# Rotary embedding on a quarter of each head: a partition that holds two runs of 8 rows instead of one of 16, with tables of 8 rows

## The chip, the cores and the metric

One core of a Trainium2 chip runs the kernel. The metric is the device time of one execution in microseconds (us); less is better. Work is spread over the engines of the core (here VectorE, called DVE in the profile, does all the arithmetic; SyncE, called SP, and GpSimd, called POOL, issue transfers) and over 16 DMA engines that move data between the device's main memory (HBM) and the 128 partitions of on-chip memory.

## What is computed

The input `x` has shape 16 x 512 x 16 x 64 (batch, sequence, heads, dim) in float32, 33.6 MB. The first 32 of the 64 values of each head are rotated, the last 32 are passed through. `cos` and `sin` have 512 x 32 values, of which the first 16 columns are used.

```python
def reference(x, cos, sin):
    batch, seq, heads, dim = x.shape
    half_dim = dim // 2
    x1, x2 = (x[..., :half_dim].copy(), x[..., half_dim:].copy())
    cos = cos[None, :, None, :].copy()
    sin = sin[None, :, None, :].copy()
    rotated_first = x1[..., :half_dim // 2] * cos[..., :half_dim // 2] - x1[..., half_dim // 2:] * sin[..., :half_dim // 2]
    rotated_second = x1[..., :half_dim // 2] * sin[..., :half_dim // 2] + x1[..., half_dim // 2:] * cos[..., :half_dim // 2]
    return np.concatenate([rotated_first, rotated_second, x2], axis=-1).astype(np.float32)
```

## The kernel before

A row is one position of one sequence: 16 heads x 64 values, 4 KB. There are 16 x 512 = 8192 rows. The kernel cuts them into T = 4 tiles of 2048 rows (8.4 MB each); in a tile, each of the 128 partitions holds K = 16 consecutive rows, 64 KB that are contiguous in HBM (`xf` and `of`, lines 36 and 37). A ring of three tile slots (`ring`, line 45) holds the tiles in on-chip memory. A tile is loaded whole, its first halves of the heads are rotated in place, and the slot is stored whole: so all of `x`, the part that passes through too, goes in and out once. Tile 3 takes the slot of tile 0 after the store of tile 0.

All loads are issued from SP's queue, and the stores of tiles 0, 1 and 3 too; the store of tile 2 is issued from POOL's. Each queue keeps its program's order. On SP this order is: load 0, load 1, the upper half (rows 8 to 15 of each partition) of load 2; then store 0, the lower half of load 2, load 3, store 1, store 3. Store 1 is held back by a dependency written by hand (lines 118 to 123) until the rotation named `near`, rows 0 to 4 of tile 2, is done. An issue on SP that has to wait holds back those behind it.

The tables: 512 positions are 32 groups of 16 rows, so partition p needs the cos and sin of group p mod 32. Two transfers from POOL's queue put the 32 groups of cos and sin on every fourth partition of `stage` (lines 62 to 64, after a memset of the columns that are read). VectorE then builds `table` on all 128 partitions: one shuffle within blocks of 32 partitions (line 73), four copies that gather the 32 groups on partitions 0 to 31 (`packed`, line 80), and four copies that write them to the four blocks of 32 partitions, each value block doubled (line 83). `C` and `Sn` are views of `table`.

`rotate(t, lo, hi)` (line 90) treats rows lo to hi of every partition of tile t with four VectorE instructions: x1 times sin into a temporary `b_t` (line 96), x1 times cos in place (97), a subtraction on the first 16 values (98) and an addition on the next 16 (101). It is called twice per tile with 8 rows, three times for tile 2 (8, 5 and 3 rows). A rotation waits for the load of its rows as a whole.

Of the kernel before, what the change touches and what calls it, by code (L numbers as in the profile page):

```python
# [1 line left out]

# [4 lines left out]


@with_exitstack
def kernel(  # L10
    ctx: ExitStack,
    tc: tile.TileContext,
    x: bass.AP,
    cos: bass.AP,
    sin: bass.AP,
    out: bass.AP,
):
    nc = tc.nc
    fp32 = mybir.dt.float32
    P = 128  # L20
    B, S, H, D = x.shape
    Q = D // 4
    HF = D // 2

    K = 16
    T = B * S // (P * K)
    PB = S // K
    REP = P // PB  # L30
    R = H * D
    NS = 3
    KC = K // 2
    KM = 5

    xf = x.rearrange("b s h d -> (b s h d)").rearrange("(t p f) -> t p f", t=T, p=P)
    of = out.rearrange("b s h d -> (b s h d)").rearrange("(t p f) -> t p f", t=T, p=P)
    cosf = cos.rearrange("(p k) j -> p (k j)", k=K)
    sinf = sin.rearrange("(p k) j -> p (k j)", k=K)

    const_pool = ctx.enter_context(tc.tile_pool(name="const", bufs=1))
    b_pool = ctx.enter_context(tc.tile_pool(name="bp", bufs=1, space=bass.MemoryType.PSUM))


    ring = const_pool.tile([P, NS, K, H, D], fp32)
    stage = const_pool.tile([P, 2, K, HF], fp32)
    spun = const_pool.tile([P, 2 * K, Q], fp32)
    packed = const_pool.tile([PB, 2 * K, Q], fp32)
    table = const_pool.tile([P, 2, K, 2, Q], fp32)

    def rows(t, lo, hi):
        return ring[:, t % NS, lo:hi].rearrange("p k h d -> p (k h d)")

    def load(t, lo=0, hi=K):
        return nc.sync.dma_start(out=rows(t, lo, hi), in_=xf[t, :, lo * R : hi * R])

    def store(t, lo=0, hi=K, queue=nc.sync):
        return queue.dma_start(out=of[t, :, lo * R : hi * R], in_=rows(t, lo, hi))  # L58


    nc.vector.memset(stage[:, :, :, 0:Q], 0.0)  # L61
    spread = stage.rearrange("(j b) t k i -> j b t (k i)", b=REP)
    nc.gpsimd.dma_start(out=spread[:, 0, 0], in_=cosf)  # L63
    nc.gpsimd.dma_start(out=spread[:, 0, 1], in_=sinf)  # L64
    load(0)
    load(1)
    load(2, KC, K)

    PQ = PB // REP
    nc.vector.stream_shuffle(  # L73
        out=spun[:],
        in_=stage.rearrange("p t k j -> p (t k) j")[:, :, 0:Q],
        mask=[j % PQ * REP for j in range(PB)],
    )
    for q in reversed(range(REP)):
        n = PQ * (q + 1)
        nc.vector.tensor_copy(out=packed[0:n], in_=spun[q * PB : q * PB + n])  # L80

    for r in range(REP):
        nc.vector.tensor_copy(  # L83
            out=table[r * PB : (r + 1) * PB].rearrange("p t k c j -> p (t k) c j"),
            in_=packed.unsqueeze(2).to_broadcast((PB, 2 * K, 2, Q)),
        )
    C = table[:, 0].rearrange("p k c j -> p k (c j)")
    Sn = table[:, 1].rearrange("p k c j -> p k (c j)")

    def rotate(t, lo, hi):  # L90
        x1 = ring[:, t % NS, lo:hi, :, 0:HF]
        c = C[:, lo:hi].unsqueeze(2).to_broadcast((P, hi - lo, H, HF))
        s = Sn[:, lo:hi].unsqueeze(2).to_broadcast((P, hi - lo, H, HF))
        b_full = b_pool.tile([P, KC, H, HF], fp32, name="b_t")
        b_t = b_full[:, 0 : hi - lo]
        nc.vector.tensor_mul(out=b_t, in0=x1, in1=s)  # L96
        nc.vector.tensor_mul(out=x1, in0=x1, in1=c)  # L97
        nc.vector.tensor_sub(  # L98
            out=x1[:, :, :, 0:Q], in0=x1[:, :, :, 0:Q], in1=b_t[:, :, :, Q:HF]
        )  # L100
        return nc.vector.tensor_add(  # L101
            out=x1[:, :, :, Q:HF], in0=x1[:, :, :, Q:HF], in1=b_t[:, :, :, 0:Q]
        )

    rotate(0, 0, KC)
    rotate(0, KC, K)
    store(0)
    load(2, 0, KC)
    load(3)
    rotate(1, 0, KC)  # L110
    rotate(1, KC, K)
    behind_loads = store(1)
    rotate(2, KC, K)
    near = rotate(2, 0, KM)
    rotate(2, KM, KC)
    store(2, queue=nc.gpsimd)

    tc.add_manual_dep(
        behind_loads.ins,
        near.ins.name,  # L120
        mybir.DependencyInfo(mybir.DependencyClass.Sync, mybir.DependencyReason.DATA),
        reason="the store follows the loads at the DMA engines",
    )
    rotate(3, 0, KC)
    rotate(3, KC, K)
    store(3)


# [1 line left out]
_INS = ['x', 'cos', 'sin']  # L130
_OUTS = [((16, 512, 16, 64), 'float32')]


# [23 lines left out]
```

## Time and profile before

| | |
|---|---|
| median of 3 runs | 161.76 us (161.6 to 161.9) |
| span of the profiled execution | 159.5 us |
| VectorE busy | 112.9 us, 47 instructions |
| GpSimd busy | 1.9 us |
| data moved | 67.24 MB, mean 422 GB/s |
| rotation of 8 rows on VectorE | 4.43 + 4.42 + 2.29 + 2.28 us |
| first rotation starts, last one ends | 23.03 us, 131.2 us |

The span is the time from the first to the last instruction of one profiled execution. The times of the runs are taken without the profiler and hold some 2 us more. In the profile a line such as `49.92 0.35 SPq L58 DMA_DIRECT2D out_dram<-ring  x1` gives the start, the length, the queue, the line of the kernel, the operation and what goes where; the length of such an issue is that of the instruction, not of the transfer. The view of the DMA queues gives, for each queue (q1 is SP's, q0 is POOL's), the number of packets, the MB and the time that its packets took as a share of 16 engines over the stretch asked for; a packet is counted in the stretch in which it starts, so a short stretch can show over 100%. Each transfer also ends with one 4-byte packet per DMA engine that reports its end: the 176 packets under 512 B are those of 11 transfers.

### The profile page before, as it was taken

Reading aid. Unit: us, or ns where it says so; the run is one execution under the profiler, and the core shown is the slowest. Engines: PE = TensorE matmul, PEld = TensorE weight load, DVE = VectorE, ACT = ScalarE, POOL = GpSimd, SP = SyncE. Lnnn points to the kernel's source line nnn. Section 1 sums busy time; section 2 is a strip of 40 time slices with the busy share of each in tenths; the row PEclk is TensorE's granted clock in tenths of the full one; section 3 lists DMA queues with packets and bytes.
Section 4 is the critical chain, followed back from the end, with each engine's and each line's share of the span. In section 5 each row is a group of like instructions: output and inputs, shape, how many; then the busy total and the mean of one; then the engine's idle time right before and its main releaser. Section 6 shows DMA issues by size and latency. Waiting matters only on the chain.

```text
span 159.5 us, 115 instructions
## 1 busy us (share of the span) xinstructions
DVE 112.9 (71%) x47; POOL 1.9 (1%) x7
## 2 busy tenths in 40 slices
DVE  1000959999999999999999999999999990000000
POOL 3000000000000000000000000010000000000000
DMA  7969979799699699699996996996996997999966
GB/s 263 542 263 542 444 345 526 345 444 526 271 493 551 279 510 526 263 394 411 510 526 263 526 526 263 526 526 263 526 526 263 526 460 329 526 394 394 526 263 263
DMA packets 1360, 67.24 MB, mean 422 GB/s; under 512 B 176, under 2 KB 176, under 8 KB 208
## 3 DMA queue, kind: packets, MB, share of 16 engines
q1 hardware_dynamic: 1152, 58.72, 85.7%
q0 software_dynamic: 208, 8.52, 12.4%
HBM read 33.69 MB, written 33.55 MB: 422 GB/s over the span
## 4 chain that ended last, share of the span: by engine, by line
DVE 61%; DMA 14%; issue 5%; DVEq 1%
DVE b_t L96 22%; DVE ring L97 22%; DMA ring<-in_x_dram 14%; DVE ring L101 10%; DVE ring L98 7%; DVEq L152 1%; DVEq L96 0%
## 5 line engine op out<-in xcount | busy, mean ns | idle before, releaser
L96 DVE TENSOR_TENSOR b_t<-ring,table 128x4096 f32<-128x4096 f32 (+2 forms) x9 | 35.6, 3959 | 2.1 <-DMA ring<-in_x_dram 1.8
L97 DVE TENSOR_TENSOR ring<-ring,table 128x4096 f32<-128x4096 f32 (+2 forms) x9 | 35.5, 3950 | 0.3
L98 DVE TENSOR_TENSOR ring<-ring,b_t 128x2048 f32<-128x2048 f32 (+2 forms) x9 | 18.4, 2049 | 0.3
L101 DVE TENSOR_TENSOR ring<-ring,b_t 128x2048 f32<-128x2048 f32 (+2 forms) x9 | 18.4, 2043 | 0.0
L73 DVE LOAD_MASK_SELECT spun<-stage x1 | 0.0, 14 | 14.4 <-DMA stage<-in_sin_dram 14.4
L83 DVE COPY table<-packed 32x1024 f32<-32x1024 f32 x4 | 2.7, 684 | 0.1
L58 POOL DMA_DIRECT2D out_dram<-ring x1 | 0.6, 562 | 101.7 <-DVE ring L101 101.7
L80 DVE COPY packed<-spun 32x512 f32<-32x512 f32 (+3 forms) x4 | 1.7, 416 | 0.1
L61 DVE MEMSET stage<- 128x512 f32 x1 | 0.5, 485 | 0.9 <-PEq L141 0.9
L73 DVE STREAM_SHUFFLE spun<-stage 128x512 f32<-128x512 f32 x1 | 0.7, 721 | 0.0
L63 POOL DMA_DIRECT2D stage<-in_cos_dram x1 | 0.6, 644 | 1.3 <-DVE stage L61 1.3
L64 POOL DMA_DIRECT2D stage<-in_sin_dram x1 | 0.5, 535 | 0.0
L141 POOL MEMSET const-bfloat16-1.0<- 128x1 bf16 x1 | 0.1, 102 | 0.0
L141 POOL MEMSET const-float32-0.0<- 128x1 f32 x1 | 0.1, 99 | 0.2 <-issue 0.2
L141 POOL MEMSET const-float32-1.0<- 128x1 f32 x1 | 0.1, 99 | 0.0
L141 POOL MEMSET const-uint8-127<- 128x1 uint8 x1 | 0.1, 99 | 0.0
## 6 DMA issues: line engine op xcount, KB each, us to landing
ring<-in_x_dram SPq DMA_DIRECT2D x2, 4096.0 KB, 40.7
stage<-in_cos_dram POOLq DMA_DIRECT2D x1, 64.0 KB, 9.0
stage<-in_sin_dram POOLq DMA_DIRECT2D x1, 64.0 KB, 13.3
ring<-in_x_dram SPq DMA_DIRECT2D x3, 29.0
out_dram<-ring SPq DMA_DIRECT2D x3, 27.4
out_dram<-ring POOLq DMA_DIRECT2D x1, 39.5
```

Source lines behind the costliest of these rows:

```text
L58: return queue.dma_start(out=of[t, :, lo * R : hi * R], in_=rows(t, lo, hi))
L61: nc.vector.memset(stage[:, :, :, 0:Q], 0.0)
L63: nc.gpsimd.dma_start(out=spread[:, 0, 0], in_=cosf)
L64: nc.gpsimd.dma_start(out=spread[:, 0, 1], in_=sinf)
L73: nc.vector.stream_shuffle(out=spun[:], in_=stage.rearrange("p t k j -> p (t k) j")[:, :, 0:Q], mask=[j % PQ * REP for j in range(PB)],)
L80: nc.vector.tensor_copy(out=packed[0:n], in_=spun[q * PB : q * PB + n])
L83: nc.vector.tensor_copy(out=table[r * PB : (r + 1) * PB].rearrange("p t k c j -> p (t k) c j"), in_=packed.unsqueeze(2).to_broadcast((PB, ...
L96: nc.vector.tensor_mul(out=b_t, in0=x1, in1=s)
L97: nc.vector.tensor_mul(out=x1, in0=x1, in1=c)
L98: nc.vector.tensor_sub(out=x1[:, :, :, 0:Q], in0=x1[:, :, :, 0:Q], in1=b_t[:, :, :, Q:HF])
L101: return nc.vector.tensor_add(out=x1[:, :, :, Q:HF], in0=x1[:, :, :, Q:HF], in1=b_t[:, :, :, 0:Q])
L152: with _tile.TileContext(nc) as tc:
```

## The change

A partition now holds, of each tile, two runs of K = 8 rows: a tile is still 2048 rows, but it is cut into two halves of 1024 rows (4 MB), and partition p holds rows 8p to 8p+7 of each half. In HBM the two runs of a partition lie 4 MB apart, and adjacent partitions 32 KB apart instead of 64 KB. In on-chip memory the layout of a slot is as large as before (`[P, NS, NI, K, H, D]` with NI = 2).

Since 8 x 64 = 512, partition p now needs the table of group p mod 64, and both runs of a partition need the same one. The tables have 8 rows on 64 partitions: the transfers put 64 groups of 1 KB on every second partition of `stage`; memset and shuffle work on half the elements; `packed` and its four copies are gone. Five copies build `table`: for each of the two blocks of 32 groups, one of 32 and one of 16 partitions straight from the shuffled tile, and at last one from partitions 0 to 63 to 64 to 127.

The whole-tile loads and stores carry both runs of each partition in one transfer (128 x 2 x 8192 values); the two half loads of tile 2 now carry one run each. The rotations have the same sizes and the same order, and so do the issues on both queues.

```diff
-    K = 16
-    T = B * S // (P * K)
+    K = 8
+    NI = 2
+    T = B * S // (P * K * NI)
     PB = S // K
-    REP = P // PB
+    G = 32
...
-    xf = x.rearrange("b s h d -> (b s h d)").rearrange("(t p f) -> t p f", t=T, p=P)
-    of = out.rearrange("b s h d -> (b s h d)").rearrange("(t p f) -> t p f", t=T, p=P)
+    xf = x.rearrange("b s h d -> (b s h d)").rearrange("(t i p f) -> t p i f", t=T, i=NI, p=P)
+    of = out.rearrange("b s h d -> (b s h d)").rearrange("(t i p f) -> t p i f", t=T, i=NI, p=P)
...
-    ring = const_pool.tile([P, NS, K, H, D], fp32)
+    ring = const_pool.tile([P, NS, NI, K, H, D], fp32)
...
-    packed = const_pool.tile([PB, 2 * K, Q], fp32)
...
-    def rows(t, lo, hi):
-        return ring[:, t % NS, lo:hi].rearrange("p k h d -> p (k h d)")
+    def runs(t, lo, hi):
+        return ring[:, t % NS, lo:hi].rearrange("p i k h d -> p i (k h d)")
 
-    def load(t, lo=0, hi=K):
-        return nc.sync.dma_start(out=rows(t, lo, hi), in_=xf[t, :, lo * R : hi * R])
+    def load(t, lo=0, hi=NI):
+        return nc.sync.dma_start(out=runs(t, lo, hi), in_=xf[t, :, lo:hi])
 
-    def store(t, lo=0, hi=K, queue=nc.sync):
-        return queue.dma_start(out=of[t, :, lo * R : hi * R], in_=rows(t, lo, hi))
+    def store(t, lo=0, hi=NI, queue=nc.sync):
+        return queue.dma_start(out=of[t, :, lo:hi], in_=runs(t, lo, hi))
...
-    spread = stage.rearrange("(j b) t k i -> j b t (k i)", b=REP)
+    spread = stage.rearrange("(m b) t k i -> m b t (k i)", b=2)
     nc.gpsimd.dma_start(out=spread[:, 0, 0], in_=cosf)
     nc.gpsimd.dma_start(out=spread[:, 0, 1], in_=sinf)
     load(0)
     load(1)
-    load(2, KC, K)
+    load(2, 1, 2)
...
-        mask=[j % PQ * REP for j in range(PB)],
+        mask=[j % (G // 2) * 2 for j in range(G)],
     )
-    for q in reversed(range(REP)):
-        n = PQ * (q + 1)
-        nc.vector.tensor_copy(out=packed[0:n], in_=spun[q * PB : q * PB + n])
-
-    for r in range(REP):
-        nc.vector.tensor_copy(
-            out=table[r * PB : (r + 1) * PB].rearrange("p t k c j -> p (t k) c j"),
-            in_=packed.unsqueeze(2).to_broadcast((PB, 2 * K, 2, Q)),
-        )
+    flat = table.rearrange("p t k c j -> p (t k) c j")
+    for g in range(PB // G):
+        for q, n in ((2 * g + 1, G), (2 * g, G // 2)):
+            nc.vector.tensor_copy(
+                out=flat[g * G : g * G + n],
+                in_=spun[q * G : q * G + n].unsqueeze(2).to_broadcast((n, 2 * K, 2, Q)),
+            )
+    nc.vector.tensor_copy(out=flat[PB:P], in_=flat[0:PB])
...
-    def rotate(t, lo, hi):
-        x1 = ring[:, t % NS, lo:hi, :, 0:HF]
+    def rotate(t, i, lo=0, hi=K):
+        x1 = ring[:, t % NS, i, lo:hi, :, 0:HF]
...
-    load(2, 0, KC)
+    load(2, 0, 1)
     load(3)
-    rotate(1, 0, KC)
-    rotate(1, KC, K)
+    rotate(1, 0)
+    rotate(1, 1)
     behind_loads = store(1)
-    rotate(2, KC, K)
-    near = rotate(2, 0, KM)
-    rotate(2, KM, KC)
+    rotate(2, 1)
+    near = rotate(2, 0, 0, KM)
+    rotate(2, 0, KM, K)
     store(2, queue=nc.gpsimd)
...
```

More of the change, by code (lines that the diff above doesn't have):

```diff
@@ L23 @@
     HF = D // 2
-    K = 16
-    T = B * S // (P * K)
+    K = 8
+    NI = 2
+    T = B * S // (P * K * NI)
     PB = S // K
-    REP = P // PB
+    G = 32
     R = H * D
     NS = 3
-    KC = K // 2
     KM = 5
-    xf = x.rearrange("b s h d -> (b s h d)").rearrange("(t p f) -> t p f", t=T, p=P)
-    of = out.rearrange("b s h d -> (b s h d)").rearrange("(t p f) -> t p f", t=T, p=P)
+    xf = x.rearrange("b s h d -> (b s h d)").rearrange("(t i p f) -> t p i f", t=T, i=NI, p=P)
+    of = out.rearrange("b s h d -> (b s h d)").rearrange("(t i p f) -> t p i f", t=T, i=NI, p=P)
     cosf = cos.rearrange("(p k) j -> p (k j)", k=K)
@@ L66 @@
     load(1)
-    load(2, KC, K)
-    PQ = PB // REP
+    load(2, 1, 2)
     nc.vector.stream_shuffle(
@@ L75 @@
         in_=stage.rearrange("p t k j -> p (t k) j")[:, :, 0:Q],
-        mask=[j % PQ * REP for j in range(PB)],
+        mask=[j % (G // 2) * 2 for j in range(G)],
     )
-    for q in reversed(range(REP)):
-        n = PQ * (q + 1)
-        nc.vector.tensor_copy(out=packed[0:n], in_=spun[q * PB : q * PB + n])
-    for r in range(REP):
-        nc.vector.tensor_copy(
-            out=table[r * PB : (r + 1) * PB].rearrange("p t k c j -> p (t k) c j"),
-            in_=packed.unsqueeze(2).to_broadcast((PB, 2 * K, 2, Q)),
-        )
+    flat = table.rearrange("p t k c j -> p (t k) c j")
[6 more added lines that the diff above has]
+    nc.vector.tensor_copy(out=flat[PB:P], in_=flat[0:PB])
     C = table[:, 0].rearrange("p k c j -> p k (c j)")
     Sn = table[:, 1].rearrange("p k c j -> p k (c j)")
-    def rotate(t, lo, hi):
-        x1 = ring[:, t % NS, lo:hi, :, 0:HF]
+    def rotate(t, i, lo=0, hi=K):
+        x1 = ring[:, t % NS, i, lo:hi, :, 0:HF]
         c = C[:, lo:hi].unsqueeze(2).to_broadcast((P, hi - lo, H, HF))
         s = Sn[:, lo:hi].unsqueeze(2).to_broadcast((P, hi - lo, H, HF))
-        b_full = b_pool.tile([P, KC, H, HF], fp32, name="b_t")
+        b_full = b_pool.tile([P, K, H, HF], fp32, name="b_t")
         b_t = b_full[:, 0 : hi - lo]
@@ L103, in rotate @@
         )
-    rotate(0, 0, KC)
-    rotate(0, KC, K)
+    rotate(0, 0)
+    rotate(0, 1)
     store(0)
-    load(2, 0, KC)
+    load(2, 0, 1)
     load(3)
-    rotate(1, 0, KC)
-    rotate(1, KC, K)
+    rotate(1, 0)
+    rotate(1, 1)
     behind_loads = store(1)
-    rotate(2, KC, K)
-    near = rotate(2, 0, KM)
-    rotate(2, KM, KC)
+    rotate(2, 1)
+    near = rotate(2, 0, 0, KM)
+    rotate(2, 0, KM, K)
     store(2, queue=nc.gpsimd)
@@ L123 @@
     )
-    rotate(3, 0, KC)
-    rotate(3, KC, K)
+    rotate(3, 0)
+    rotate(3, 1)
     store(3)
```

## The prediction

> **What bounds the kernel now.** I read the page first: the engine table, the 40 slices and the DMA queues.
>
> ```profile
> span 159.5 us, 115 instructions
> DVE 112.9 (71%) x47; POOL 1.9 (1%) x7
> DMA packets 1360, 67.24 MB, mean 422 GB/s; under 512 B 176, under 2 KB 176, under 8 KB 208
> q1 hardware_dynamic: 1152, 58.72, 85.7%
> q0 software_dynamic: 208, 8.52, 12.4%
> ```
>
> The two queues hold the 16 DMA engines for 85.7 + 12.4 = 98.1% of the span, 156.5 of 159.5 us. The 3.0 us left over lie at the two ends: no packet starts before 1.75 us, and after the last packets (started at 155.5 to 156.0, 2.4 us long) come the last landing and the closing barrier. VectorE is busy for 71% only. So this kernel is one unbroken DMA stream, although the chain of waits puts 61% of the span on VectorE: that chain ends at the last VectorE instruction (131 us) and does not follow the queue of stores behind it. What happens on VectorE counts only where it makes a DMA issue too late to keep the stream unbroken. So I looked next at the timeline, for the start and the issues:
>
> ```profile
> 0.74 1.33 SPq L55 DMA_DIRECT2D ring<-in_x_dram  x3
> 15.83 0.01 DVE L73 LOAD_MASK_SELECT spun<-stage  x1 [14.43 <-DMA stage<-in_sin_dram]
> ...
> 18.41 2.78 DVE L83 COPY table<-packed 32x1024 f32<-32x1024 f32 x4
> 23.03 4.43 DVE L96 TENSOR_TENSOR b_t<-ring,table 128x4096 f32<-128x4096 f32 x1 [1.85 <-DMA ring<-in_x_dram]
> ...
> 49.92 0.35 SPq L58 DMA_DIRECT2D out_dram<-ring  x1
> ...
> 98.90 32.68 SPq L58 DMA_DIRECT2D out_dram<-ring  x2
> ```
>
> The tables are complete at 21.2 us, and VectorE then idles 1.85 us until load(0) has landed: the first rotation starts on the load, not on the tables. Store(0) is issued at 49.92 us, store(1) at 98.90, store(3) at 131.24.
>
> Last I asked for the packets of single stretches, because the changed kernel makes its transfers of other pieces. The trace already holds both sizes: a whole tile goes as 128 packets of 64 KB (one per partition), and each half of tile 2 as 128 packets of 32 KB. The first two rows below are stretches with whole tiles only (24 to 41 us and 82 to 97 us), the third one with the first half of tile 2 only (43 to 50 us); columns are packets, MB, share of 16 engines.
>
> ```profile
> q1 hardware_dynamic: 112, 7.34, 99.6%
> ...
> q1 hardware_dynamic: 96, 6.29, 96.7%
> ...
> q1 hardware_dynamic: 87, 2.85, 94.2%
> ```
>
> Packets are counted where they start. A 64 KB packet takes 0.996 x 17 x 16 / 112 = 2.4188 us, and 0.967 x 15 x 16 / 96 = 2.4175 us; I take 2.418. A 32 KB packet takes 0.942 x 7 x 16 / 87 = 1.2127 us. Two of them take 2.4254, that is 7 ns more than one of 64 KB (5 to 10 ns with the rounding of the shares). That is the only price of the smaller piece that this trace shows.
>
> **The change part by part.**
>
> *Tables (off the path).* Removed on VectorE: four copies of about 0.416 us into packed (1.66) and four of 0.684 into table (2.74). The memset and the shuffle work on half the elements (0.485 and 0.721 us before). Added: five copies of 512 elements, each between half of 0.684 (0.34) and the 0.418 of the 32x512 copy, 1.7 to 2.1 us in all. Some 2.3 to 2.7 us of copies go, and up to 0.6 us of shuffle and memset. All of that falls in the wait for load(0), so it is worth nothing: VectorE idles longer. Even if the sin table landed no earlier than now (15.83), the tables would be ready by 15.83 + 0.72 + 2.1 = 18.7, 4.3 us ahead of the load. The table transfers become 64 rows of 1 KB instead of 32 rows of 2 KB, the same 128 KB; their whole share today is 32 packets of 4 KB, about 0.3 us per engine, and I see no reason for a change above 0.1. They probably land earlier, as they take turns with 32 KB packets instead of 64 KB ones. That too is hidden.
>
> *Rotations.* Same forms, same order, same count: 0.
>
> *Loads and stores of whole tiles.* Seven issues (loads 0, 1, 3; stores 0 to 3) x 128 partitions / 16 = 56 packets of 64 KB per engine become 112 of 32 KB. The two halves of tile 2 keep one run per partition. Cost: 56 x 7.2 ns = 0.40 us, straight on the end, since the stream has no gap that could take it. Bounds: 0, if two runs of a partition travel as one packet; 0.28 to 0.56 by the rounding; 0.82 by the other half of tile 2, whose reads follow the stores (71.5 to 79 us: 96 packets, 97.3%, 1.2163 us each, so 56 x 14.6 ns). No row shows a 32 KB store, but a 64 KB store is priced like a load (140 to 157 us: 112 packets, 99.7%, 2.421 us), so I give both the same. I take 0.40, since most of the packets follow packets of their own direction.
>
> *The 4 MB between two runs.* No row shows such a step. The nearest ones are tiles whose partitions lie 64 KB apart, on which 16 engines read and write at 2.418 us per packet without a slow one, so the memory side has room: 0. From far above, each jump could cost what the first packets of the run cost (below, 0.75 us): 56 x 0.75 = 42 us. I take 0, because adjacent partitions are already separate requests at 64 KB steps, and pay nothing.
> The Trainium skill speaks against the change here: "DMA: Bandwidth & Descriptors", section "Latency and other measured facts", reports copies whose partitions lie a large power of two apart, with 207 GB/s at 512 KB and 103 at 4 MB. Taken at its word, the 135 us of whole-tile packets would double, an estimate of some 297 us from that page. But its distance is that between partitions, which here shrinks from 64 to 32 KB; no run here shows a 4 MB one.
>
> *Issues.* The order on SP and on POOL stays: loads 0, 1, half of 2; store 0; other half; load 3; stores 1 and 3 on SP; tables and store 2 on POOL. Each whole-tile issue now describes 256 runs, not 128. SP's five load issues take 0.33 to 0.43 us now. Whether that grows is not shown; between 0 and a doubling, +0.35 us. What matters is when the stream needs the next issue:
> - Start: issue at 0.74, first packets at 1.75 to 2.6. Any growth counts in full.
> - Store(0): issue at 49.92; the last half-tile packets end, and its own start, at 50.9 to 51.7. The lead is about 1.0 us, as at the start, so there is hardly any slack today. Load end moves by 16 x 7 ns = 0.11 later, VectorE (through load(0)'s landing) by 8 x 7 = 0.06: slack grows 0.05.
> - Store(1): issue at 98.90 behind the rotation marked near; its packets start at 99.8 to 100.3, where the loads end. Load end moves 32 x 7 = 0.23, VectorE 0.06: slack grows 0.17.
> - Load(3) (71.72) is covered by the half of tile 2 that runs until 80.5; store(2) on POOL (issue 0.56 us) by store(1), alone good for 19 us; store(3) (131.24) by store(2)'s packets, up to about 143. No cost there, and nothing else waits behind them.
> I take 0, because POOL's issues do not go by the runs they describe: 0.54 to 0.64 us for a table of 32, 0.56 for a store of 128.
>
> **Sum**: the profiled 159.5 + 0.40 = 159.9 us. The median of the runs is 161.76, 2.26 above that span; the same offset gives 162.16, rounded 162.2.
>
> **The rivals.**
> - *Nothing changes* (the two runs travel together, or the 7 ns hide): 161.8. For it: 7 ns is near the rounding of the view. Against: the half-tile stretches show each run of 32 KB as a packet of its own.
> - *Later issues*: describing two runs per partition takes SP 0.35 us longer, and the stream breaks at the start (0.35), at store(0) (0.35 - 0.05) and at store(1) (0.35 - 0.17). For it: both leads are only about 1 us. Against: POOL's rows. 162.16 + 0.83 = 163.0.
> - *Memory side*: 4 MB steps slow some packets. At the price of the read-after-write row, 162.6; further up the sum has no row but the 42 us, 204.
> - *Faster, through the start.* The first 16 packets take 372.5% x 0.85 us = 3.17 us each instead of 2.42, 0.75 us of excess on every engine. If that belongs to the length of the first request and vanishes with shorter ones, 161.76 + 0.40 - 0.75 = 161.4. It shows as faster only if nearly all of it goes. Against: this looks like the delay to the first data, which any length pays.
>
> **How the numbers follow.** My forecast (0.40, give or take 0.2: 161.95 to 162.4) gets 0.57, nothing 0.14, later issues 0.15, the memory side 0.06, faster 0.08. 0.2% is 0.32 us, about what a measurement of this kernel tells from no change: slower begins at 162.08, faster below 161.44. The lower edge of the forecast falls within; so faster 0.08, same 0.22, slower 0.70. The range goes from 161.6 (nothing, less the 0.16 by which runs lie under the median) to 163.1 (later issues, with 0.1 of scatter); it leaves out most of the faster case and the upper part of the memory one.
>
> **What would show it.** Right: q1 has 1152 + 6 x 128 = 1920 packets, q0 208 + 128 = 336; whole-tile stretches give 1.213 us per packet; the shares sum to about 98% of a span near 159.9; the first rotation still starts near 23.1 behind load(0), with over 4 us of idle in front. Wrong: packets of 64 KB still (nothing); windows around 1.75, 51 or 100 us in which less than 16 engines are at work (later issues); packets clearly above 1.22 us in mid-stream (memory side); first packets under 1.5 us (faster). An issue on SP well over 0.43 us would make the second rival likely.

## The result, and the profile after

The changed kernel takes 163.49 us (median of 4 runs, 163.02 to 164.04), the kernel before 161.68 us (161.54 to 161.9, 4 runs): a ratio of 1.0117, 95% interval 1.0095 to 1.014. It is slower, as forecast, but by 1.8 us and not by 0.4, and outside the range that was given (161.6 to 163.1). A second set of 6 runs gave 163.83 us (163.19 to 164.51) and 1.0137 (1.0117 to 1.0158). The runs of the changed kernel also scatter over 1.5 us, those of the kernel before over some 0.6.

The page of the changed kernel, with the engine table and the DMA queues:

```profile
span 160.9 us, 112 instructions
DVE 110.1 (68%) x44; POOL 2.1 (1%) x7
DMA packets 2256, 67.24 MB, mean 418 GB/s; under 512 B 176, under 2 KB 176, under 8 KB 208
q1 hardware_dynamic: 1920, 58.72, 85.5%
q0 software_dynamic: 336, 8.52, 12.3%
```

The reader sees the packet counts that were forecast (1920 and 336: each whole-tile packet has become two), and the same kind of kernel: 97.8% of 160.9 us on the DMA queues, 157.3 us instead of 156.5. The span is 1.42 us longer, so 0.8 us of it is packet time and some 0.6 us is not.

The timeline of the changed kernel, at its start and at the issues on SP:

```profile
10.99 0.01 DVE L69 LOAD_MASK_SELECT spun<-stage  x1 [9.86 <-DMA stage<-in_sin_dram]
...
13.29 0.42 DVE L81 COPY table<-table 64x512 f32<-64x512 f32 x1
23.09 4.43 DVE L91 TENSOR_TENSOR b_t<-ring,table 128x4096 f32<-128x4096 f32 x1 [9.39 <-DMA ring<-in_x_dram]
...
49.98 0.39 SPq L57 DMA_DIRECT2D out_dram<-ring  x1
...
98.97 32.72 SPq L57 DMA_DIRECT2D out_dram<-ring  x2
```

The tables are complete at 13.7 us instead of 21.2 and the first rotation starts at 23.09 instead of 23.03: all that the shorter table work gained is waiting for load 0 (9.39 us of idle in front of the rotation instead of 1.85). The issues are 0.06 to 0.07 us later. None of this is a loss of more than that.

Where packets do nothing but follow each other, they cost what the half tile had shown. The queue view of the changed kernel from 110 to 128 us, where stores 1 and 2 take turns (packets, MB, share of 16 engines):

```profile
q0 software_dynamic: 127, 4.16, 53.5%
q1 hardware_dynamic: 113, 3.70, 47.6%
```

1.011 x 18 x 16 / 240 = 1.213 us for 32 KB. Over the run, 112 packets of 1.213 instead of 56 of 2.418 make 0.45 us.

The rest stands at one place, the turn from store 0 to the half load of tile 2 that is queued behind it. First the kernel before, the last packet of store 0 on each of the 16 engines (67.5 to 69 us); then the changed kernel, the same packets (69.3 to 70.5 us) and, next, the first packets of the half load (71 to 72.6 us, with 16 end-of-transfer packets of 7 to 9 ns among the 32):

```profile
q1 hardware_dynamic: 16, 1.05, 184.3%
```

```profile
q1 hardware_dynamic: 16, 0.52, 141.4%
...
q1 hardware_dynamic: 32, 0.52, 97.3%
```

In the kernel before, a last packet takes 1.843 x 1.5 = 2.76 us, 0.35 above 2.418. In the changed one it takes 1.414 x 1.2 = 1.70 us, 0.48 above 1.213, and the first reads take 0.973 x 1.6 = 1.56 us, 0.34 above. I summed, from the packet records, all time above the standing price (2.418 and 1.213 us) in packets that start between 60 and 77 us: 0.41 us per engine in the kernel before (0.43 in a second trace), 0.86 in the changed one (1.11 in a second). This sum is called "the turn" below. In no other stretch does the excess come to more than 0.05 us per engine, but for the first packets of the run (0.75 before, 0.66 after).

The last term is at the end. The stretches of the kernel before and of the changed one in which the last packets start (us, length, busy VectorE, busy GpSimd, clock, DMA share, GB/s):

```profile
155.50:156.50 1.00, 0.00 (x0) 0.00 (x0) 1.00 2.42 1049
156.50:157.50 1.00, 0.00 (x0) 0.00 (x0) 1.00 0.00 0
```

```profile
156.00:157.00 1.00, 0.00 (x0) 0.00 (x0) 1.00 1.06 459
157.00:158.00 1.00, 0.00 (x0) 0.00 (x0) 1.00 1.14 492
158.00:159.00 1.00, 0.00 (x0) 0.00 (x0) 1.00 0.31 131
```

Before, all 16 last packets start in one stretch (1049 GB/s for 1 us are 16 x 64 KB). After, 4 engines (131 GB/s are 4 packets of 32 KB) start theirs after 158 us, the other twelve before. By the end-of-transfer packets, the last engine ends 0.62 us after the mean of the 16, before 0.14. The trace lines up as: packets +0.45, turn +0.45, uneven end +0.48, first packet 0.06 later; in all 1.44 of 1.42 us. What is left out nearly cancels. The engines also stand still at the turn, 0.23 us per engine between 71 and 72.5 us (in the kernel before under 0.01). Against that, each packet starts 3 to 4 ns before the one ahead of it has ended, which happens 56 times more often (some -0.2), and the first packets of the run are 0.09 us cheaper.

The second trace of the changed kernel (span 162.3 us) shows the uneven end more plainly:

```profile
157.00:158.00 1.00, 0.00 (x0) 0.00 (x0) 1.00 1.06 459
158.00:159.00 1.00, 0.00 (x0) 0.00 (x0) 1.00 0.38 164
159.00:160.00 1.00, 0.00 (x0) 0.00 (x0) 1.00 0.08 33
```

One packet of 32 KB is 33 GB/s for 1 us: one engine alone is still at work, 1.89 us after the mean. Its own packets can be followed back one by one: at the turn its last store packet takes 2.29 us, it stands still for 0.41 us, and its first read takes 2.27 us: 2.5 us lost within 5 us. It never makes them up: behind 81 us all 16 engines have about 64 packets of 32 KB left, the late one as many as the others. When the others change to store 1 at 100 us it loses another 0.6 us on its last two reads. Of the 2.83 us by which this trace is longer than that of the kernel before, the uneven end makes 1.74, the slow packets at the turn 0.70 and the smaller pieces 0.45 (the rest -0.06): in this slower run the late engine is the main term.

### The profile page after: what moved, and what is told of

The parts are those of the page before. It is cut to its first block, busy times and chain, and to the rows that moved or that the text cites. A ratio compares the mean times of both kernels' runs of the same rounds, so it can differ in the third digit from the quotient of the medians.

```text
span 160.9 us, 112 instructions
## 1 busy us (share of the span) xinstructions
DVE 110.1 (68%) x44; POOL 2.1 (1%) x7
## 3 DMA queue, kind: packets, MB, share of 16 engines
q1 hardware_dynamic: 1920, 58.72, 85.5%
## 4 chain that ended last, share of the span: by engine, by line
DVE 61%; DMA 14%; issue 5%; DVEq 1%
DVE b_t L91 22%; DVE ring L92 22%; DMA ring<-in_x_dram 14%; DVE ring L96 10%; DVE ring L93 7%; DVEq L147 1%; DVEq L91 0%
## 5 line engine op out<-in xcount | busy, mean ns | idle before, releaser
L77 DVE COPY table<-spun 32x512 f32<-32x512 f32 (+1 forms) x4 | 1.7, 417 | 0.1
```

What stands on the lines that cost most here:

```text
L77: nc.vector.tensor_copy(out=flat[g * G : g * G + n], in_=spun[q * G : q * G + n].unsqueeze(2).to_broadcast((n, 2 * K, 2, Q)),)
```

## Experiments

Each run is compared with the kernel before on the same chip (161.56 to 161.70 us there). "Last engine" is its end after the mean of the 16 in the trace of that run. In the diffs, names are those of the kernel before unless the changed kernel is meant, and only the lines that matter are shown ("..." between them). In e9, e13, e14, e15 and e17 tile 0 is rotated in the order upper half, lower half.

**The changed kernel again, and three versions of where its runs lie.**

> The changed kernel once more, for the scatter and a second trace. In its first trace the extra time stands in three terms: 32 KB packets at 1.213 us instead of 64 KB ones at 2.418 (0.45 us), slow packets at the turn from store 0 to the reads of tile 2 at 69 to 73 us (a mean of 0.85 us per DMA engine instead of 0.41), and an uneven end (last engine 0.61 us after the mean instead of 0.14). If the slow turn belongs to the kernel, this trace shows it again: 0.7 to 1.8 us per engine of excess there, and times of 162.8 to 164.2 us. If it was chance in one execution, the excess falls to about 0.4 and the time to about 162.3.

Measured (e1): 163.83 us, turn 1.11, last engine 1.89 us. The slow turn belongs to the kernel. How uneven it leaves the engines differs from run to run (last engine 0.62 us late at 163.09 us, 1.89 at 164.51), which fits the scatter.

```diff
+    PAD = 16
-    ring = const_pool.tile([P, NS, K, H, D], fp32)
+    ring = const_pool.tile([P, NS, 2, KC * R + PAD], fp32)
```

> The kernel before with 16 unused values between the two halves of a slot, so that each partition's 64 KB travel as two 32 KB pieces that are adjacent in HBM; rows, tables and order as before. Theory A (the size of the piece does it all): 32 KB packets at 1.213 us, a slow turn of 0.7 to 1.2 us per engine, 163.0 to 164.0 us, like the changed kernel. Theory B (the 4 MB between the runs makes the turn slow, the size only its 0.45 us): turn at about 0.4 us, 162.1 to 162.3 us.

Measured (e2): 163.98 us (1.0155, 1.0135 to 1.0174), turn 1.01, last engine 1.68. Some 0.4 us of the time is something else: an issue for slots with a gap takes 0.60 to 0.66 us on SP, and the first packet comes at 2.21 us instead of 1.75 (in e10 and e14 too, at 2.17 and 2.18).

```diff
-        return nc.sync.dma_start(out=runs(t, lo, hi), in_=xf[t, :, lo:hi])
+        for i in range(lo, hi):
+            nc.sync.dma_start(out=runs(t, i, i + 1), in_=xf[t, :, i : i + 1])
...
-    rotate(0, 0)
     rotate(0, 1)
+    rotate(0, 0)
```

> The changed kernel with every whole-tile transfer cut into two of 4 MB, one for each run, so that no transfer alternates between places 4 MB apart; packets stay at 32 KB and partitions 32 KB apart. Tile 0 is rotated in the order second run, first run, so that VectorE starts after the whole of load 0 as before. Theory A (size of the piece): turn still 0.7 to 1.2 us per engine, 163.0 to 164.0 us. Theory B (the alternation over 4 MB): turn back at about 0.4 us, 162.2 to 162.5 us (0.45 for the packets, at most 0.1 for the added end-of-transfer packets).

Measured (e3): 164.35 us (1.017, 1.0157 to 1.0183), turn 1.02, last engine 1.02. It also lost 0.8 us at 92 to 94 us, which I had not planned: the first half of store 2 went out from POOL at 90.74 us, while load 3 was still running.

```diff
-    load(2, 1, 2)
+    load(2, 0, 1)
...
-    load(2, 0, 1)
+    load(2, 1, 2)
```

> The changed kernel with the two half loads of tile 2 exchanged: the first run is loaded at the start, the second one behind store 0. Only the addresses at the turn change, by 4 MB. Theory A and theory B both expect no difference (162.8 to 164.2 us, turn 0.7 to 1.8 us). A third theory C, that particular addresses of the read and the written tile collide at the turn, expects another turn: 0.4 us or less, or clearly over 1.8, and a time at least 0.4 us away from the changed kernel's.

Measured (e4): 163.27 us (163.09 to 164.78), turn 1.02, last engine 1.62.

What follows: the 4 MB between the runs is without effect. With adjacent runs (e2) the loss is as large, and without alternation (e3) too. Moving the addresses at the turn by 4 MB (e4) leaves the turn at 1.02; the median of e4 is 0.56 us below that of e1, less than the runs of either scatter. Theory B and theory C fall; the cause is in cutting the transfers into smaller pieces.

**Which pieces: store 0, the reads behind it, or the other tiles.** In e6 the slots of tiles 1 and 2 have the gap of e2, the slot of tiles 0 and 3 has none; e10 is the reverse.

```diff
-    store(0)
+    store(0, 0, KC)
+    store(0, KC, K)
```

> The kernel before with store 0 alone cut into two transfers of 32 KB pieces; all else in 64 KB as before. Theory A1 (the pieces of the store that comes right ahead of the turn make it slow): turn of 0.7 to 1.2 us per DMA engine, a last engine 0.4 to 2 us behind the mean, 162.2 to 163.9 us. Theory A2 (small pieces everywhere are needed, for instance because they leave the engines in another state long before the turn): turn at 0.4 us, 161.5 to 161.9 us.

Measured (e5): 162.77 us (1.0071, 1.0058 to 1.0084), but the turn from store 0 to the reads is 0.00; the loss lies at the other end of store 0. The view of SP's issues in this run, and the queue view for 50 to 51 us, the last packets of the loads ahead of store 0:

```profile
36.55 13.79 SPq L58 DMA_DIRECT2D out_dram<-ring  x2
```

```profile
q1 hardware_dynamic: 16, 0.52, 204.5%
```

The first half of store 0 is issued as soon as half of tile 0 is rotated, 14 us before the loads ahead of it are through. Their last packets take 2.05 us each instead of 1.213, on all engines alike. The kernel before issues store 0 at 49.92 us, 1.0 us before its first packet, and its loads end at full speed. This run mixed two things and settles neither theory. It shows one thing more: the reads behind store 0 are issued as early as in the kernel before (50.39 us, before 50.31), and the turn to them costs nothing.

```diff
+    whole = const_pool.tile([P, 2, KC * R], fp32)
+    split = const_pool.tile([P, NS - 1, 2, KC * R + PAD], fp32)
```

> The kernel before with a gap in the slots of tiles 1 and 2 alone: load 1, store 1 and store 2 go in 32 KB pieces, load 0, store 0, load 3 and store 3 in 64 KB pieces. Theory A1: turn at 0.4 us, only 24 packets per engine are split, 0.19 us, so 161.7 to 162.0 us. Theory A2: the turn is slow, 162.5 us or more.

Measured (e6): 162.03 us (161.74 to 163.19 over 12 runs; 1.0043, 1.0026 to 1.0061). Six of the twelve runs lie where theory A1 puts them and one just above (162.11); three took 162.5 and two 163.2, where theory A2 has them. In the traced one (162.5 us) the turn was 0.56 and one engine 0.64 late. So a kernel with load 0 and store 0 in whole pieces can lose too, and neither theory covers all runs.

```diff
-    load(2, 0, KC)
+    load(2, 0, 4)
+    load(2, 4, KC)
```

> The kernel before with the half load behind store 0 cut into two transfers of 16 KB pieces. Theory A1: no change beyond 0.1 us, 161.5 to 161.9 us, turn at 0.4 us. Theory A3 (the pieces of the reads at the turn count just as well): turn of 0.7 us or more per engine, 162.2 us or more.

Measured (e7): 161.76 us (1.0014, 1.0005 to 1.0022), turn 0.39. The pieces of the reads behind the turn do not count; theory A3 falls.

```diff
-    store(0)
+    for k in range(0, K, 4):
+        store(0, k, k + 4)
```

> The kernel before with store 0 cut into four transfers of 16 KB pieces. Theory A1 with a dose: turn at least as slow as with halves, 0.8 to 2 us per engine, 162.4 to 165 us. Theory A1 without a dose: like halves. Theory A2: 161.6 to 162.0 us.

Measured (e8): 163.01 us, again with nothing at the turn and 1.0 us where the early half of store 0 meets the loads, as in e5.

**Store 0 in small pieces without the early issue, the slot of tile 0, and the turn taken apart.**

```diff
-    rotate(0, 0, KC)
     rotate(0, KC, K)
-    store(0)
+    rotate(0, 0, KC)
+    store(0, 0, KC)
+    store(0, KC, K)
```

> Like the earlier run with store 0 in two transfers of 32 KB pieces, but tile 0 is rotated in the order upper half, lower half, so that both transfers are issued at 50 us, when the tile is done; there the first was issued at 36.6 us and the slow packets moved from the end of store 0 to its beginning. Theory A1 (the pieces of the store ahead of the turn): slow packets at 69 to 74 us again, 0.7 to 1.2 us per DMA engine, 162.3 to 163.9 us. Theory A4 (what counted there was the early issue, not the pieces): 0.4 us at the turn and 161.5 to 161.9 us.

Measured (e9): 162.00 us (161.8 to 162.15; 1.0023, 1.0014 to 1.0032), turn 0.61, last engine 0.20. Between the two, and the engines stay even: the pieces of store 0 are not the loss. Whether they lengthen the turn by 0.2 us, one trace cannot tell: e16 below, which is the kernel before up to the turn, has 0.56, and e17, with the same pieces of store 0, has 0.42.

```diff
-        return split[:, t % NS - 1, :, 0 : KC * R] if t % NS else whole[:]
+        return whole[:, t % NS - 1] if t % NS else split[:, :, 0 : KC * R]
```

> The reverse of the run that split tiles 1 and 2: only the slot of tiles 0 and 3 has a gap, so load 0, store 0, load 3 and store 3 go in 32 KB pieces and load 1, store 1 and store 2 in 64 KB. Theory A1: 0.26 us for 32 packets per engine, plus a slow turn as in the changed kernel (0.7 to 1.2 us, uneven): 162.5 to 164.0 us. Theory A4: 161.8 to 162.1 us.

Measured (e10): 164.00 us (162.84 to 164.94; 1.0141, 1.0112 to 1.017), turn 0.92, last engine 2.16. Cutting the transfers of tiles 0 and 3 brings all of the loss (even without the 0.4 us of its later start), cutting those of tiles 1 and 2 (e6) little of it in the median.

```diff
-    store(0)
-    load(2, 0, 1)
+    first = store(0)
+    late = load(2, 0, 1)
+    tc.add_manual_dep(late.ins, first.ins.name, ...)
```

> The changed kernel, with the half load behind store 0 issued only when store 0 has landed. Theory M (the slow packets come from reads that start while other engines still write, because they are queued behind the writes): the last packets of store 0 return to 1.21 us, the first reads take the 0.5 to 0.8 us excess of the first packets of the run, the engines are even again (last one at most 0.3 us behind the mean), and in place of the slow packets a gap of about 1.5 us stands (landing 0.4, issue to first packet 1.0): 163.5 to 164.5 us, with less scatter than the changed kernel. If the slow packets have another cause (the stores' own last pieces), they stay in store 0's last packets and the gap comes on top: 164.5 us or more.

Measured (e11): 165.18 us (165.13 to 165.37). The stretches of this run around the turn, columns as above:

```profile
69.30:70.30 1.00, 1.00 (x1) 0.00 (x0) 1.00 1.22 524
...
71.20:72.40 1.20, 1.17 (x2) 0.00 (x0) 1.00 0.00 0
72.40:73.40 1.00, 1.00 (x1) 0.00 (x0) 1.00 1.88 524
```

With no reads queued behind it, store 0 ends at full speed (16 packets, 1.22 us each); then nothing starts for over 1.2 us; then the first 16 reads take 1.88 us, 0.66 above 1.213, the excess of the first packets of the run. Theory M has its first two signs: in the changed kernel it is the reads queued behind them that slow the last stores. They need not always do so, since in e5 and e8 reads are queued just as early and the turn costs nothing. The last engine is 0.43 us late, not 0.3, and the time is above 164.5 for another reason: the loads now end at 103 us, store 1 is issued at 99 as before, and the last reads take 0.84 us per engine more, the loss of e5 once more.

> The kernel before once more, for a second trace of its turn: all theories expect 0.3 to 0.5 us of excess per engine at 68 to 73 us and ends of the engines within 0.3 us.

Measured (e12): span 159.5 us, turn 0.43, last engine 0.25.

**Which transfer leaves the engines uneven.**

```diff
-    load(0)
+    load(0, 0, KC)
+    load(0, KC, K)
...
-    store(0)
+    store(0, 0, KC)
+    store(0, KC, K)
     load(2, 0, KC)
-    load(3)
+    load(3, 0, KC)
+    load(3, KC, K)
```

> The kernel before with load 0, store 0, load 3 and store 3 each cut into two transfers of 32 KB pieces, one half of every partition each; the same pieces as in the run with a split slot for tiles 0 and 3 (164.0 us), but no transfer carries two pieces of one partition. Theory P (the transfer that carries two pieces per partition makes the turn slow and uneven): turn at 0.4 to 0.6 us, ends within 0.4 us, 0.26 us for the packets and 0.1 for the added issues, 161.9 to 162.3 us. Theory Q (32 KB pieces in both load 0 and store 0, in whatever transfers): turn of 0.7 us or more, a last engine 1 us or more behind the mean, 162.8 us or more.

Measured (e13): 163.13 us (162.02 to 163.44; 1.0078, 1.0055 to 1.0101), turn 0.63, last engine 1.04. The turn is nearly as theory P has it (0.6 at most), the last engine and the time are as theory Q has them.

Next, the split slot of e10 with store 0 as two transfers:

```diff
-    store(0)
+    store(0, 0, 1)
+    store(0, 1, 2)
```

> The run with a split slot for tiles 0 and 3 once more, but store 0 alone goes as two transfers, one half of every partition each. Theory P, if store 0 is the transfer that counts: turn at 0.4 to 0.6 us and even, 162.0 to 162.6 us (issues of that layout are 0.25 us longer). Theory Q, or theory P with another transfer: as before, 162.8 to 164.9 us.

Measured (e14): 164.27 us (164.06 to 164.49), turn 0.80, last engine 1.37. Theory P falls for store 0; load 0 still carries two pieces per partition here, and e13 has shown late engines without such a transfer.

Next, load 0 alone, then load 3 alone:

```diff
-    load(0)
+    load(0, 0, KC)
+    load(0, KC, K)
...
-    rotate(0, 0, KC)
     rotate(0, KC, K)
+    rotate(0, 0, KC)
```

> The kernel before with load 0 alone in two transfers of 32 KB pieces. Theories P and Q: turn at 0.4 us, 161.6 to 161.9 us (0.06 for the packets). If the pieces of load 0 by themselves disturb the later turn: 162.3 us or more.

Measured (e15): 162.23 us over 12 runs, in two groups: six of 161.34 to 161.64 us, six of 162.83 to 163.98 (five of them up to 163.58). All together they cannot be told from the kernel before (1.0029, 0.9998 to 1.006). The traced run took 162.84 us: turn 0.67, last engine 1.08. Nothing but load 0 is cut here, its packets are over at 23 us, and the engines come apart at 68 to 73 us. There is no trace of a run of the faster group.

```diff
-    load(3)
+    load(3, 0, KC)
+    load(3, KC, K)
```

> The kernel before with load 3 alone in two transfers of 32 KB pieces; it is issued at 72 us, behind the turn. Theories P and Q: no change of the turn, 161.6 to 161.9 us.

Measured (e16): 161.94 us (161.83 to 162.21), turn 0.56, last engine 0.35. The time is just above the forecast. The turn is above 0.4 although nothing ahead of it was changed: by that much single traces differ.

Last, every whole-tile transfer but load 0, then load 1 alone:

```diff
-    load(1)
+    load(1, 0, KC)
+    load(1, KC, K)
...
-    store(0)
+    store(0, 0, KC)
+    store(0, KC, K)
...
-    load(3)
+    load(3, 0, KC)
+    load(3, KC, K)
...
-    behind_loads = store(1)
+    behind_loads = [store(1, 0, KC), store(1, KC, K)]
...
-    store(2, queue=nc.gpsimd)
+    store(2, 0, KC, queue=nc.gpsimd)
+    store(2, KC, K, queue=nc.gpsimd)
...
-    store(3)
+    store(3, 0, KC)
+    store(3, KC, K)
```

> The kernel before with every whole-tile transfer but load 0 in two transfers of 32 KB pieces (loads 1 and 3, stores 0 to 3), the two of a store issued together. Packets cost 48 x 8 ns = 0.38 us, added issues up to 0.1. Theory L0 (the pieces of the first transfer of the run are what makes the later turn uneven): turn 0.4 to 0.6 us, ends within 0.5 us, 162.0 to 162.4 us in every run. Theory N (every split ahead of the turn adds its share): turn of 0.7 us or more, uneven, 162.8 us or more.

Measured (e17): 163.10 us (162.93 to 163.26), turn 0.42, last engine 0.17. The turn is even and cheap although everything but load 0 is in small pieces, as theory L0 says; the time is 0.7 us above its forecast for a cause outside it. GpSimd's line of this run's timeline, and the first packets behind it (92 to 93 us):

```profile
90.54 0.56 POOL L58 DMA_DIRECT2D out_dram<-ring  x1 [87.65 <-DVE ring L102]
```

```profile
q1 hardware_dynamic: 11, 0.36, 124.0%
```

As in e3, one half of store 2 was issued at 90.5 us into the middle of load 3, and reads took 1.24 x 16 / 11 = 1.80 us; the sum of it is 0.82 us per engine. 163.10 less that is 162.3, within the forecast; this is an estimate, that version was not run.

```diff
-    load(1)
+    load(1, 0, KC)
+    load(1, KC, K)
```

> The kernel before with load 1 alone in two transfers. Theory L0: like the kernel before, 161.5 to 162.0 us in every run. Theory N: two groups of runs as with load 0 alone, some at 161.4 and some at 162.8 us or more.

Measured (e18): 161.74 us (161.54 to 162.12; 1.0008, 0.9998 to 1.0018), turn 0.18, last engine 0.16. Theory N falls.

Over all traces: the nine runs with load 0 in 32 KB pieces and the reads queued behind store 0 have their last engine 0.62 to 2.16 us behind the mean; the eight with load 0 in 64 KB pieces and store 0 issued when it was needed 0.14 to 0.35, but for e6 with 0.64. By the end-of-transfer packets, no engine is more than 0.55 us behind the mean at the end of store 0 in any of these 17 traces. At the end of the half load behind it the last engine is 0.62 to 1.42 us behind in the nine and in e6, and 0.19 to 0.38 in the other seven. So the engines come apart mainly on the reads behind the turn.

The packet records hold a second difference between the two groups, at the other end of store 0. In the nine traces and in e6, some engines stand still at 51 us, between their last load packet and their first packet of store 0: 0.01 to 0.16 us per engine in the mean, 0.03 in the changed kernel. In the other seven none does. A store 0 that reaches the engines a trace too late thus goes with engines that come apart 20 us later, and it covers e6, which the pieces of load 0 do not. No run changed this alone, so whether it is a cause or only a sign is not shown.

## Why the prediction was wrong

- *The bound.* Right. The kernel stayed one DMA stream, and the shorter table work was worth nothing: VectorE idles for it.
- *Packets.* Right: 0.40 us were forecast, 0.45 measured, 1.213 us per packet where it is not disturbed (some 0.2 of it comes back, as packets overlap by 3 to 4 ns).
- *The 4 MB between two runs.* Right at nothing: e2 loses as much without it. The page "DMA: Bandwidth & Descriptors" of the Trainium skill, section "Latency and other measured facts", puts a loss on large powers of two between partitions. The runs here, with 4 MB inside a partition and 32 KB between partitions, show none of it.
- *Issues.* Taken at nothing; the direct cost is under 0.1 us. SP's issues grew from 0.33 to 0.43 us to 0.37 to 0.47, the first packet came 0.06 us later, and a gap of 0.03 us per engine opened at store 0, none at store 1. The reason given for nothing did not hold: POOL's issue of store 2, which describes 256 runs instead of 128, grew from 0.56 to 0.73 us. The rival with later issues, which gave the range its upper end, did not happen at its price of 0.83 us. Its sign at 51 us did show, in small, and what it does to the turn was left open above.
- *The step that failed* is the end of "Loads and stores of whole tiles": "I take 0.40, since most of the packets follow packets of their own direction". I had the stretch from 71.5 to 79 us in hand, whose packets were dearer because they follow stores, used it as a bound on the price of a piece, and did not ask what the turn itself cost, nor whether it would stay as it was. It cost 0.41 us per engine already, hidden in the 98.1%. In the changed kernel it costs 0.86 and 1.11, so a term of 0.45 to 0.70 us was put at nothing.
- *A second thing missing*: I made the sum over the mean of the 16 engines. The time ends with the slowest one. In the kernel before that made 0.14 us, and nothing in its profile said that it would grow to 0.6 and 1.9 us.
- *The rival on the memory side* had a part of the mechanism (slow packets where reads meet stores), but with the jump as its cause, and at 162.6.

What is shown: the loss beyond the packets comes at the turn from store 0 to the reads queued behind it, and consists of slower packets there and of engines that leave it apart. It is due to transfers in 32 KB pieces, not to where the runs lie (e2 to e4). Of the pieces, those of load 0 alone are enough for it in half of the runs (e15), and those of all other whole tiles without load 0 are not (e17). That is not the whole rule: the other half of e15's runs are as fast as the kernel before, and five of e6's twelve runs are slow with load 0 whole.

What is open: by what way load 0, over by 23 us, acts on a turn at 70 us. The engines do not arrive more spread out: when the loads ahead of store 0 end, at 51 us, the last engine is 0.23 to 0.46 us behind the mean in all 17 traces, even or not. The short gap at the start of store 0 goes with the uneven turn without exception, but was not varied by itself. The order in which the 16 engines arrive may count too; it was not looked at. The largest turn sums, 0.8 to 1.1, occur only where load 0 carries two pieces per partition or everything is cut (e3); which parts add up there was not separated.

None of the versions beats the kernel before.

## What to carry to other kernels

When DMA engines are busy from end to end, look for the places where the stream changes direction and sum the time above the standing packet price there; a share near 100% hides it. Issue a store behind loads when it is needed and not long before (here 1 us ahead: free; 4 to 14 us ahead: 0.8 to 1.1 us per engine). Holding reads back until a store has landed costs more than it saves (e11: 165.18 us, or some 164.3 without its loss at 100 us). Read the end by the slowest engine, not by the mean. Pieces of half the size can cost more than their price of some 8 ns each: here 0.45 us of 1.8 to 2.3.

## What the runs showed of the hardware that was not expected

- A store that is issued while loads still run slows the last loads by 0.8 to 1.06 us per DMA engine (e5, e8, at the end of e11, in e3 and e17 through POOL's queue). Once both directions take turns steadily, packets are back at 1.213 us (e3, behind 95 us).
- An engine that falls behind at a turn stays behind to the end, 85 us later: in the second trace of the changed kernel one engine lost 2.5 us in 5 us and 0.6 more at the next turn.
- Reads queued behind a store need not slow it: the turn cost nothing where the first part of store 0 was issued 14 us before the loads ahead of it ended (e5, e8), 0.2 to 0.6 us per engine where it followed them without a gap, and 0.6 to 1.1 where a gap of 0.01 to 0.16 us stood in front of it.
- Cutting the first transfer alone gave two groups of runs, 161.34 to 161.64 and 162.83 to 163.98 us, with the difference, in the one trace of the slower group, arising 50 us behind that transfer.
